# Seven products of an MLP pair in three PSUM banks instead of seven

## The chip, the cores and the metric

The kernel runs on one core of a Trainium2 chip. The time is device microseconds of one execution. The kernel before took 1361.07 us (median of 3 runs, 1359.0 to 1362.8).

## The reference, cut to what matters

The program is one step of a two-layer decoder over 576 tokens (512 of a prompt, 64 of samples), 1024 features wide. A layer ends with an MLP:

```
up = rmsnorm(x, w) @ w_up            # 576 x 1024 times 1024 x 4096
x  = x + square(relu(up)) @ w_down   # 576 x 4096 times 4096 x 1024
```

Everything is float32. The kernel keeps that precision with matmuls of a narrower kind: each operand is split into a high and a low part, and a product is the sum of three matmuls (high times high, high times low, low times high).

## The kernel before, in words

Data lies with features on the 128 partitions and tokens along the free side, in two halves of 288 tokens (`TH`). The 4096 hidden features are 32 tiles of 128. A layer's MLP is a loop over eight chunks of four tiles (`fc` in `mlp`); while a chunk is computed, the chunk before it is multiplied down into x (`down`, line 1018, tile `pd`).

The first six tiles of a layer are computed plainly (`up_tile`, line 336, tile `pu`). The other 26 are taken in 13 pairs (`up_pair`). The 2 x 2 block product of a pair (two tiles of weights, two halves of tokens, the 1024 features in two halves) is done in the Strassen-Winograd way: seven products instead of eight, on sums of weights and sums of inputs. The second chunk holds one pair, and chunks three to eight hold two each. So a layer has one single pair, then six first and six second pairs of a chunk; the last of the second ones has no pair after it.

A product is 12 matmuls of 128 x 288 (four feature blocks, three matmuls each), made by the helper `mul`. The products are p1 to p7. Their right sides are parts of the normed x (`xh`, `xl`) or of the sums `Th`, `Tl`. Their left sides are weights in four kinds of tile: `a` (p1, p2), `s` (p6, p5), `b` (p7, p4), each eight blocks wide and split into `uh`, `ul`, and `d` (p3), four blocks wide, split into `vh`, `vl`. The tag `u` has three buffers, so a, s and b of one pair fill it, and the next pair's a, s and b must each wait until the last matmul on the same buffer is done.

The path of a weight tile: SyncE loads 512 KB into one of three `raw` buffers (line 312); VectorE makes the sums s and the changed ra and rb (lines 1066 to 1069); ScalarE casts the high part (`uh` or `vh`, line 1059); VectorE subtracts to get the low part (`ul` or `vl`, line 1060). When that is done, the raw buffer is free and SyncE may load the next tile.

Each product has a PSUM bank of its own, out of five that rotate (`bank`). ScalarE copies p1 out of its bank (line 1099); VectorE adds the products to what stands in SBUF (line 1089: U = p1 + p6, W = U + p5, p1 + p2, W + p7, U + p7, W + p3, and U with p7 in it + p4). Each of the four sums then gets relu and the norm's factor (line 1092), ScalarE squares it (line 1128) and splits it into high and low (`fh`, line 455; `fl`, line 456).

The order of the instructions on every engine is made by the framework's scheduler when the program is built, from the order of the code, from priorities and from estimates of its own. `high_priority(HP)` puts a piece 3000 places earlier in that ranking. At run time each engine works its list off in that order, and a semaphore wait holds up all that stands behind it on its engine.

Of the kernel before, what the change touches and what calls it, by code (L numbers as in the profile page):

```python
# [14 lines left out]
ALU = mybir.AluOpType  # L15
# [9 lines left out]
TH = T // 2  # L25
# [10 lines left out]
HP = 3000  # L36
# [111 lines left out]
class Kern:  # L148
# [903 lines left out]
    def up_pair(self, P, i, Q, rstd):  # L1052

        nc, V, S, li = self.nc, self.nc.vector, self.nc.scalar, self.li
        ra, rb = (self.raw(self.I["wu"][li, f]) for f in (2 * i, 2 * i + 1))
        hl = lambda n, w, b: (P.t(n + "h", [w, 128], F32R, b), P.t(n + "l", [w, 128], F32R, b))

        def split(hl, src):
            S.copy(hl[0], src)  # L1059
            V.tensor_tensor(hl[1], src, hl[0].bitcast(F32), op=ALU.subtract)  # L1060
            return hl

        with self.tc.high_priority(HP):
            a = split(hl("u", 8, 3), ra)
            s = P.t("s", [8, 128])
            V.tensor_tensor(s[:, :4], rb[:, :4], rb[:, 4:], op=ALU.add)
            V.tensor_tensor(s[:, 4:], s[:, :4], ra[:, :4], op=ALU.subtract)
            V.tensor_tensor(rb[:, :4], ra[:, :4], rb[:, :4], op=ALU.subtract)
            V.tensor_tensor(ra[:, 4:], ra[:, 4:], s[:, 4:], op=ALU.subtract)
            s = split(hl("u", 8, 3), s)  # L1070
            b = split(hl("u", 8, 3), rb)
            d = split(hl("v", 4, 1), ra[:, 4:])

        out = [[self.fp.t(n, dt=F32R, bufs=8) for n in ("fh", "fl")] for _ in range(2)]
        rs = [rstd[:, :TH], rstd[:, TH:]]

        def mul(n, w, o, q):
            ps = self.bank(n)
            j = 0
            for k in range(4):  # L1080
                (wh, wl), (xh, xl) = (t[:, o + k] for t in w), Q[q][k]
                for u, x in ((wh, xh), (wh, xl), (wl, xh)):
                    nc.tensor.matmul(ps[:, :TH], u, x, start=j == 0, stop=j == 11)  # L1083
                    j += 1
            return ps[:, :TH]

        def add(out, x, y):
            with self.tc.high_priority(HP):
                V.tensor_tensor(out, x, y, op=ALU.add)

        def relu(c, m, h):
            V.scalar_tensor_tensor(c, c, 0.0, rs[h], op0=ALU.max, op1=ALU.mult)
            self.square(c, out[m], h)

        U, W = P.t("U", TH), P.t("W", TH)
        p1 = mul("p1", a, 0, "B11")
        c00 = self.half_tile(P)
        with self.tc.high_priority(HP):
            S.copy(c00, p1)
        add(U, c00, mul("p6", s, 4, "T2"))  # L1100
        p5 = mul("p5", s, 0, "T1")
        add(W, U, p5)
        add(c00, c00, mul("p2", a, 4, "B21"))
        relu(c00, 0, 0)
        p7 = mul("p7", b, 0, "T3")
        c11 = self.half_tile(P)
        add(c11, W, p7)
        relu(c11, 1, 1)
        add(U, U, p7)
        c01 = self.half_tile(P)  # L1110
        add(c01, W, mul("p3", d, 0, "B22"))
        relu(c01, 0, 1)
        c10 = self.half_tile(P)
        add(c10, U, mul("p4", b, 4, "T4"))
        relu(c10, 1, 0)
        return out

    def half_tile(self, P=None):
# [256 lines left out]
```

## Time and profile before

| | |
|---|---|
| median of 3 runs | 1361.07 us |
| the profiled execution's own time | 1359.7 us |
| its span | 1357.2 us |
| TensorE busy | 1334.6 us (98%) |
| VectorE busy | 1031.6 us (76%) |
| ScalarE busy | 651.4 us (48%) |

The profile is of one execution. PE is TensorE's matmuls, PEld its weight loads, DVE VectorE, ACT ScalarE, POOL GpSimd and SP SyncE. Matmuls overlap, so their durations (0.29 us here) sum to more than the time that they take; the distance from start to start is what counts. The MLP of layer 0 lies at 292 to 680 us of the span, that of layer 1 at 958 to 1347 us; the first and the last matmul of pairs are at 331 and 629 us in the one, 997 and 1295 us in the other.

### The profile page before, as it was taken

To read this page: it belongs to the slowest core of one execution; us is meant where nothing else is said; L and a number is where in the kernel's file an instruction comes from. 1 tells how busy PE (TensorE), PEld (TensorE's weight loads), DVE (VectorE), ACT (ScalarE), POOL (GpSimd) and SP (SyncE) were. 2 spreads that over 40 slices of the span, in tenths; PEclk is the share of its full clock that TensorE was granted. 3 is DMA by queue.
4 is the path that set the end of the run, shared out by engine and by line. 5 is a ranking of instruction groups with operands and counts; after the bars stand their busy time and mean duration, and the time that the engine had idled before them with its cause. 6 is when DMAs were issued, how large, how long until landed. Compare 5 with 4: busy or idle time off the path is not lost.

```text
span 1357.2 us, 25456 instructions
## 1 busy us (share of the span) xinstructions
PE 1334.6 (98%) x10376; PEld 1287.3 (95%) x10376; DVE 1031.6 (76%) x2059; ACT 651.4 (48%) x1167; POOL 63.7 (5%) x125
## 2 busy tenths in 40 slices
PE   7999999999999999999999999999999999999997
PEld 7898999899999999999998999989999999999997
DVE  7977887498678677777669789766877778677755
ACT  6456446666243234333454653666653243334325
POOL 4020102000000000000100010010000000000000
PEclk9999999999999999999999999999999999999999
DMA  7142424123223232322431332141223223222312
GB/s 262 48 159 105 148 76 143 48 78 110 78 66 106 78 100 72 124 68 82 145 120 37 112 133 80 65 139 61 80 79 125 73 69 109 78 93 79 116 57 70
DMA packets 39716, 131.33 MB, mean 97 GB/s; under 512 B 5960, under 2 KB 8128, under 8 KB 39568
## 3 DMA queue, kind: packets, MB, share of 16 engines
q1 hardware_dynamic: 29312, 102.12, 22.0%
q0 software_dynamic: 6544, 22.65, 4.8%
q10 hardware_dynamic: 3744, 4.95, 1.1%
q8 instruction: 81, 1.33, 0.4%
q14 instruction: 35, 0.29, 0.1%
HBM read 120.32 MB, written 11.34 MB: 97 GB/s over the span
## 4 chain that ended last, share of the span: by engine, by line
PE 92%; DVE 4%; ACT 3%; issue 1%; DMA 0%; DVEq 0%; ACTq 0%
PE pd L336 34%; PE p L1083 21%; PE pi L336 18%; PE pu L336 6%; PE sc L550 2%; PE pl L1235 2%; PE ss L399 1%; PE pdt L336 1%; PE ao L351 1%; PE pt L983 1%; PE o L351 1%; ACT hi L323 1%; PE lg L959 1%; PE y L351 1%; DVE lo L323 0%
## 5 line engine op out<-in xcount | busy, mean ns | idle before, releaser
L336 PE MATMUL pd<-fh,hi 128*128 128x288 f32 x960 | 283.8, 296 | 0.0
L336 PE MATMUL pd<-fl,hi 128*128 128x288 f32 x960 | 283.7, 296 | 0.0
L336 PE MATMUL pd<-fh,lo 128*128 128x288 f32 x960 | 283.6, 295 | 0.0
L323 ACT CAST hi<-raw 128x1024 fp32r<-128x1024 f32 x134 | 140.4, 1048 | 290.4 <-PE pd L336 156.6
L336 PE MATMUL pi<-xh,hi 128*128 128x288 f32 x704 | 210.5, 300 | 7.4 <-ACT xh L374 7.4
L336 PE MATMUL pi<-xl,hi 128*128 128x288 f32 x704 | 211.1, 300 | 0.7 <-DVE xl L375 0.7
L336 PE MATMUL pi<-xh,lo 128*128 128x288 f32 x704 | 210.4, 299 | 0.0
L1018 DVE TENSOR_TENSOR x<-x,pd 128x288 f32<-128x288 f32 x240 | 108.1, 451 | 101.3 <-PE pd L336 101.2
L323 DVE TENSOR_TENSOR lo<-raw,hi 128x1024 fp32r<-128x1024 f32 x134 | 163.9, 1223 | 25.0 <-ACT hi L323 24.1
L336 PEld LDWEIGHTS pd<-fh,hi 128*128 128x128 f32 x960 | 181.1, 189 | 0.0
L336 PEld LDWEIGHTS pd<-fl,hi 128*128 128x128 f32 x960 | 181.0, 189 | 0.0
L336 PEld LDWEIGHTS pd<-fh,lo 128*128 128x128 f32 x960 | 180.6, 188 | 0.0
L336 PEld LDWEIGHTS pi<-xh,hi 128*128 128x128 f32 x704 | 133.1, 190 | 11.1 <-ACT xh L374 7.4
L336 PEld LDWEIGHTS pi<-xh,lo 128*128 128x128 f32 x704 | 133.2, 189 | 3.9 <-issue 3.3
L336 PEld LDWEIGHTS pi<-xl,hi 128*128 128x128 f32 x704 | 133.2, 189 | 3.0 <-DVE xl L375 1.2
L1083 PE MATMUL p<-Th,ul 128*128 128x288 f32 x312 | 92.0, 295 | 0.0
L1083 PE MATMUL p<-Th,uh 128*128 128x288 f32 x312 | 92.0, 295 | 0.0
L1083 PE MATMUL p<-Tl,uh 128*128 128x288 f32 x312 | 92.0, 295 | 0.0
L1083 PE MATMUL p<-xh,ul 128*128 128x288 f32 x312 | 91.9, 294 | 0.0
L1083 PE MATMUL p<-xl,uh 128*128 128x288 f32 x312 | 91.7, 294 | 0.0
L1083 PE MATMUL p<-xh,uh 128*128 128x288 f32 x312 | 91.7, 294 | 0.0
L1059 ACT CAST uh<-raw 128x1024 fp32r<-128x1024 f32 x52 | 54.5, 1047 | 66.6 <-PE p L1083 43.2
(487 smaller groups left out, 3025.5 us busy)
## 6 DMA issues: line engine op xcount, KB each, us to landing
raw<-in_wu SPq DMA_DIRECT2D x64, 512.0 KB, 3.2
raw<-in_wd SPq DMA_DIRECT2D x64, 512.0 KB, 4.4
raw<-in_wi SPq DMA_DIRECT2D x44, 512.0 KB, 3.3
raw<-in_wo SPq DMA_DIRECT2D x16, 512.0 KB, 3.2
x<-in_xT SPq DMA_DIRECT2D x8, 288.0 KB, 6.4
a<-acd ACTq DMA_DIRECT2D x4, 576.0 KB, 4.3
xl<-in_xT POOLq DMA_DIRECT2D x8, 288.0 KB, 4.1
xd<-x POOLq DMA_DIRECT2D x8, 288.0 KB, 2.4
```

The lines of the kernel that those rows point to most:

```text
L323: self.split_ins = nc.scalar.copy(hi, raw).ins, nc.vector.tensor_tensor(lo, raw, hi.bitcast(F32), op=ALU.subtract).ins
L336: self.nc.tensor.matmul(out, w, x[:, a], start=n == 0, stop=n == last)
L351: self.nc.tensor.matmul(out, w, x, start=n < 2, stop=n >= len(products) - 2, skip_group_check=True)
L399: nc.tensor.matmul(ps[:, :TH], ones, s[:, TH * h : TH * h + TH], start=n == 0, stop=n == len(sqs) - 1)
L550: nc.tensor.matmul(pv[:, :, 64 * ci : 64 * ci + 64], kE[:, 128 * ci : 128 * ci + 128], qE[:, :, 64 * ci : 64 * ci + 64], start=True, stop= ...
L959: nc.tensor.matmul(lg[i][:, e, :n], Q[e][kv(i), a], K[kv(i), s0 : s0 + n], start=True, stop=True)
L983: nc.tensor.transpose(pt[:, e, 128 * k : 128 * k + 128], l[:, 128 * k : 128 * k + 128], self.ident)
L1018: self.nc.vector.tensor_tensor(y[:, a], x[:, a], ps, op=ALU.add)
L1059: S.copy(hl[0], src)
L1083: nc.tensor.matmul(ps[:, :TH], u, x, start=j == 0, stop=j == 11)
L1235: nc.tensor.matmul(ps, u[:, o + q], v[:, a], start=j == 0, stop=j == 11)
```

## The change

The seven products go to three banks. In bank A, p1, p6, p5 and p3 are accumulated on top of each other: only p1's first matmul starts the bank anew (`start`), and only p3's last one ends the sum (`stop`). After p1, after p6 and after p5 ScalarE copies what the bank holds to SBUF (`keep`): U1 = p1, U = p1 + p6, W = p1 + p6 + p5. What is in A after p3 is W + p3, one of the four outputs. Bank C takes p7, which is read once for W + p7, and then p4 on top of it, read for U + p7 + p4. Bank B takes p2. The order of the products becomes p1, p2, p6, p7, p5, p3, p4; it was p1, p6, p5, p2, p7, p3, p4.

A pair has three ScalarE copies where it had one, and three VectorE adds where it had seven. The relu step of W + p3 reads the bank itself. U1 is one more SBUF tile of 288 floats per partition, and `dynamic_dma_scratch_size=8192` sets the SBUF kept for descriptors of GpSimd's DMAs, which was left at its default of 16384 bytes.

```diff
-        def mul(n, w, o, q):
-            ps = self.bank(n)
+        def mul(ps, w, o, q, last=True, first=True):
+
             j = 0
             for k in range(4):
                 (wh, wl), (xh, xl) = (t[:, o + k] for t in w), Q[q][k]
                 for u, x in ((wh, xh), (wh, xl), (wl, xh)):
-                    nc.tensor.matmul(ps[:, :TH], u, x, start=j == 0, stop=j == 11)
+                    nc.tensor.matmul(ps, u, x, start=first and j == 0, stop=last and j == 11, skip_group_check=True)
                     j += 1
-            return ps[:, :TH]
-
-        def add(out, x, y):
+
+        def keep(dst, ps):
             with self.tc.high_priority(HP):
-                V.tensor_tensor(out, x, y, op=ALU.add)
-
-        def relu(c, m, h):
-            V.scalar_tensor_tensor(c, c, 0.0, rs[h], op0=ALU.max, op1=ALU.mult)
+                S.copy(dst, ps)
+
+        def done(m, h, x, y=None):
+            c = self.half_tile(P)
+            with self.tc.high_priority(HP):
+                if y is not None:
+                    V.tensor_tensor(c, x, y, op=ALU.add)
+                    x = c
+                V.scalar_tensor_tensor(c, x, 0.0, rs[h], op0=ALU.max, op1=ALU.mult)
             self.square(c, out[m], h)
 
-        U, W = P.t("U", TH), P.t("W", TH)
-        p1 = mul("p1", a, 0, "B11")
-        c00 = self.half_tile(P)
-        with self.tc.high_priority(HP):
-            S.copy(c00, p1)
-        add(U, c00, mul("p6", s, 4, "T2"))
-        p5 = mul("p5", s, 0, "T1")
-        add(W, U, p5)
-        add(c00, c00, mul("p2", a, 4, "B21"))
-        relu(c00, 0, 0)
-        p7 = mul("p7", b, 0, "T3")
-        c11 = self.half_tile(P)
-        add(c11, W, p7)
-        relu(c11, 1, 1)
-        add(U, U, p7)
-        c01 = self.half_tile(P)
-        add(c01, W, mul("p3", d, 0, "B22"))
-        relu(c01, 0, 1)
-        c10 = self.half_tile(P)
-        add(c10, U, mul("p4", b, 4, "T4"))
-        relu(c10, 1, 0)
+
+        A, B, C = (self.bank(n)[:, :TH] for n in ("pA", "pB", "pC"))
+        U1, U, W = P.t("U1", TH), P.t("U", TH), P.t("W", TH)
+        mul(A, a, 0, "B11", last=False)
+        keep(U1, A)
+        mul(B, a, 4, "B21")
+        done(0, 0, U1, B)
+        mul(A, s, 4, "T2", last=False, first=False)
+        keep(U, A)
+        mul(C, b, 0, "T3", last=False)
+        mul(A, s, 0, "T1", last=False, first=False)
+        keep(W, A)
+        done(1, 1, W, C)
+        mul(A, d, 0, "B22", first=False)
+        done(0, 1, A)
+        mul(C, b, 4, "T4", first=False)
+        done(1, 0, U, C)
         return out
...
-    nc = _bacc.Bacc("TRN2", target_bir_lowering=False, num_devices=1)
+    nc = _bacc.Bacc("TRN2", target_bir_lowering=False, num_devices=1, dynamic_dma_scratch_size=8192)
```

TensorE, before, a second pair of a chunk (layer 0, fourth chunk), where p5 ends (bank `p_814`) and p2 begins in another bank:

```order
L1083 MATMUL p_814_5638<-xl_3429,uh_5591 128x288
L1083 MATMUL p_814_5638<-xh_3428,ul_5592 128x288
L1083 MATMUL p_815_5652<-xh_3408,uh_5582 128x288 [waits DVE_49]
L1083 MATMUL p_815_5652<-xl_3409,uh_5582 128x288
L1083 MATMUL p_815_5652<-xh_3408,ul_5583 128x288
```

TensorE, now, the same pair, where p5 ends in bank A (`pA_5577`) and p3 begins in it:

```order
L1083 MATMUL pA_5577<-xl_3429,uh_5561 128x288
L1083 MATMUL pA_5577<-xh_3428,ul_5562 128x288
L336 MATMUL pd_5699<-fh_4890,hi_5695 128x288
L336 MATMUL pd_5699<-fl_4891,hi_5695 128x288
L336 MATMUL pd_5699<-fh_4890,lo_5696 128x288
L336 MATMUL pd_5699<-fh_4892,hi_5695 128x288
L336 MATMUL pd_5699<-fl_4893,hi_5695 128x288
L336 MATMUL pd_5699<-fh_4892,lo_5696 128x288
L1083 MATMUL pA_5577<-xh_3408,vh_5569 128x288 [waits Activation_49]
L1083 MATMUL pA_5577<-xl_3409,vh_5569 128x288
```

The scheduler has moved six matmuls of the down product (`pd`) into the place between p5 and p3, and p3's first matmul has a wait on ScalarE. In the first pair of a chunk ten matmuls of the second pair's p1 stand in that place; in the single pair and in a layer's last pair there are four of `pd`.

ScalarE, before, the same chunk, from the copy of the first pair's p1 (`T1a_5472`) to the copy of the second pair's p1 (`T_5622`); between them stand the casts of the second pair's weights:

```order
L1099 COPY T1a_5472<-p_783_5459 128x288 [waits PE_49]
L1059 CAST uh_5582<-raw_5578 128x1024 [waits DMAHW0_49,DVE_49,PE_49]
L323 CAST hi_5792<-raw_5790 128x1024 [waits DMAHW3_49]
L1059 CAST uh_5591<-s_5586 128x1024 [waits DVE_49,PE_49]
L1059 CAST vh_5599<-raw_5578 128x512 [waits DVE_49,PE_49,Activation_49]
L1059 CAST uh_5595<-raw_5580 128x1024 [waits DMAHW1_49,PE_49]
L1099 COPY T_5622<-p_811_5609 128x288 [waits PE_49]
```

ScalarE, now, in the first pair of that chunk (`pA_5432`), its copies of U and of W:

```order
L1088 COPY U_5436<-pA_5432 128x288 [waits PE_49]
L323 CAST hi_5757<-raw_5755 128x1024 [waits DMAHW3_49]
L1059 CAST uh_5561<-s_5556 128x1024 [waits PE_49]
L1088 COPY W_5437<-pA_5432 128x288 [waits PE_49]
L1059 CAST vh_5569<-raw_5548 128x512 [waits DVE_49,PE_49]
```

And in the second pair (`pA_5577`):

```order
L1059 CAST uh_5565<-raw_5550 128x1024 [waits DMAHW1_49,PE_49]
L1088 COPY U_794_5580<-pA_5577 128x288 [waits PE_49]
L1128 ACTIVATE u_5542<-u_5542 128x288 [waits DVE_49]
L455 CAST fh_5430<-u_5542 128x288 [waits Activation_49]
L1088 COPY U_5581<-pA_5577 128x288 [waits PE_49]
L1128 ACTIVATE T_5608<-T_5608 128x288 [waits DVE_49]
L455 CAST fh_5573<-T_5608 128x288 [waits Activation_49]
L1059 CAST uh_5945<-raw_5941 128x1024 [waits DMAHW6_49]
L1088 COPY W_5582<-pA_5577 128x288 [waits PE_49]
```

The copy of W stands right behind a cast of 1024 elements in both: in the first pair behind the cast of the second pair's s (`uh_5561`, which waits for a matmul), in the second pair behind the cast of the next chunk's first weight tile (`uh_5945`, which waits for its load). Outside the pairs the lists of all engines read as before.

## Rows read from the trace of the kernel before

**Rows 1.** The page: busy time of each engine, share of the span, instructions.

```profile
PE 1334.6 (98%) x10376; PEld 1287.3 (95%) x10376; DVE 1031.6 (76%) x2059; ACT 651.4 (48%) x1167; POOL 63.7 (5%) x125
```

**Rows 2.** PE's waits over the span: waited for, us in total, times, longest.

```profile
PE pi L336 <- ACT xh L374: 7.4, 1, 7.4
PE xt L746 <- DVE b L727: 1.9, 2, 1.5
...
PE sc L550 <- DVE qE L546: 0.3, 1, 0.3
```

**Rows 3.** Busy time in both stretches of pairs: length, engines (instructions), PE clock, DMA, GB/s.

```profile
331.00:660.00 329.00, 329.00 (x2481) 329.00 (x2480) 239.28 (x439) 120.06 (x199) 3.33 (x6) 1.00 0.26 87
1000.00:1290.00 290.00, 290.00 (x2186) 290.00 (x2186) 218.31 (x399) 108.55 (x180) 0.00 (x0) 1.00 0.27 90
```

**Rows 4.** Timeline of PE, a pair's p3, p4 and the next p1: start, us.

```profile
375.88 0.30 PE L1083 MATMUL p<-xh,vh 128*128 128x288 f32 x1
...
377.48 0.30 PE L1083 MATMUL p<-Th,uh 128*128 128x288 f32 x1
...
379.08 0.29 PE L1083 MATMUL p<-xh,uh 128*128 128x288 f32 x1
...
380.53 0.29 PE L1083 MATMUL p<-xh,ul 128*128 128x288 f32 x1
380.65 0.30 PE L1083 MATMUL p<-Th,uh 128*128 128x288 f32 x1
```

**Rows 5.** Timeline of ACT, the copy of that p1.

```profile
380.85 0.40 ACT L1099 COPY u<-p 128x288 f32<-128x288 f32 x1 [0.66 <-PE p L1083]
```

**Rows 6.** Timeline around a start of PE after ACT, late in the span.

```profile
1348.07 0.44 ACT L1245 ACTIVATE sq<-x 128x288 f32<-128x288 f32 x1 [0.58 <-DVE x L1239]
...
1348.56 0.30 PEld L1249 LDWEIGHTS ss<-sq,ones 128*128 128x128 f32 x2 [0.80 <-ACT sq L1245]
```

**Rows 7.** Timeline of PE, a matmul after a short gap and the one behind it.

```profile
778.48 0.40 PE L336 MATMUL pi<-xl,hi 128*128 128x288 f32 x1
778.72 0.29 PE L336 MATMUL pi<-xh,lo 128*128 128x288 f32 x1
```

**Rows 8.** Timeline of ACT, a cast that waited for its load, and what follows it.

```profile
430.49 0.75 ACT L455 CAST fh<-u 128x288 fp32r<-128x288 f32 x2
...
434.05 1.05 ACT L1059 CAST uh<-raw 128x1024 fp32r<-128x1024 f32 x1 [1.47 <-DMA raw<-in_wu]
435.00 0.44 ACT L1128 ACTIVATE T1b<-T1b 128x288 f32<-128x288 f32 x1
```

**Rows 9.** Timelines of DVE and of SP before that cast.

```profile
428.15 1.22 DVE L1060 TENSOR_TENSOR ul<-raw,uh 128x1024 fp32r<-128x1024 f32 x1
429.28 0.82 DVE L1092 SCALAR_TENSOR_TENSOR u<-u,ssq 128x288 f32<-128x288 f32 x2
...
426.76 1.46 SPq L312 DMA_DIRECT2D raw<-in_wd  x2
429.39 0.33 SPq L312 DMA_DIRECT2D raw<-in_wu  x1
```

**Rows 10.** The page's DMA issues: tile, queue, count, KB, median us from issue to landing.

```profile
raw<-in_wu SPq DMA_DIRECT2D x64, 512.0 KB, 3.2
```

**Rows 11.** ACT's waits for that load: us in total, times, longest.

```profile
ACT uh L1059 <- DMA raw<-in_wu: 22.5, 13, 3.5
```

**Rows 12.** Line 1089 on DVE, one of its forms: min/median/max ns.

```profile
L1089 DVE TENSOR_TENSOR U<-U,p x26: 445/447/449, 340.1 to 1292.6; 128x288 f32<-128x288 f32 x26
```

**Rows 13.** The page's queue of GpSimd's DMAs: packets, MB, share.

```profile
q0 software_dynamic: 6544, 22.65, 4.8%
```

## The prediction

> **What bounds the kernel now.** I read the busy times first: TensorE is busy 98% of the span, no other engine over 76% [rows 1]. The list of TensorE's waits has nine rows, 14.3 us in total, and no row of a pair's matmuls (line 1083) is among them [rows 2]. Then the two stretches in which the pairs stand: TensorE is busy in all of 329.0 and all of 290.0 us, at a granted clock of 1.00, with 2481 and 2186 matmuls [rows 3]. That is 0.1326 us from one matmul's start to the next. So in the pairs nothing can be won by waiting less: TensorE waits for nothing. Time changes only if TensorE is made to wait, or if the 0.1326 us change.
>
> **What the change removes.** Four VectorE adds of a pair go, 26 x 4 = 104 instructions of 0.447 us [rows 12], about 46 us of VectorE's busy time. VectorE is busy 239.28 of 329.0 us there [rows 3] and holds up no matmul, so this is worth nothing: TensorE's own stream is the cover, and it stays. Seven banks a pair become three; as no product waited for a bank, that is worth nothing either. The number and shape of matmuls stay. The smaller reserve for GpSimd's transfers touches 6544 packets, 4.8% of the transfer engines' time [rows 13]; nearly all of it lies in the mixers, and I cost it at nothing. If TensorE did wait there, one such wait would be in the size of those that it has, up to 7.4 us [rows 2].
>
> **What it adds.** ScalarE gets two more copies a pair, 52 of 0.40 us [rows 5]: 21 us on an engine that is busy 120.06 of 329.0 us [rows 3]. Their own time is hidden. New is that TensorE waits for them: p6, p5 and p3 go on in bank A and may start only when the copy out of A is done. Behind a waiting matmul the whole of TensorE stands. I work out each of the three waits from one chain. The last matmul of a product starts 0.133 before the place S that follows it, and lasts 0.29. In the trace p1's last matmul starts at 380.53, ends at 380.82, and the copy starts at 380.85 [rows 4, 5]: 0.03 later. The copy takes 0.40. From ScalarE's end to TensorE's next weight load it is 0.05 (1348.07 + 0.44 = 1348.51, load at 1348.56) [rows 6]. After a gap the first matmul shares its time with its weight load: the next one starts 0.24 later (778.48 to 778.72) in place of 0.133 [rows 7], 0.11 more. Together: the sum goes on at S + 0.16 + 0.03 + 0.40 + 0.05 + 0.11 = S + 0.75, if ScalarE is free. What stands between must cover 0.75 us, which takes 5.7 matmuls.
>
> *p6 after the copy of U1, p5 after the copy of U.* Between them stand p2 and p7, 12 matmuls each, 1.59 us: covered, with 0.84 to spare. ScalarE's list puts a cast of 1024 elements ahead of the copy of U1 in second pairs; it is released by the end of p4 of the pair before and eats this margin to about nothing (below 0.02 x 12 = 0.2). I take 0.1 us.
>
> *p3 after the copy of W.* Between p5 and p3 stands only what the scheduler moved there: 4, 10 or 6 matmuls.
>
> Four of `pd`, the single pair and the last pair of each layer, 4 pairs: nothing stands ahead of the copy on ScalarE. 4 x 0.1327 = 0.53, needed 0.75: a wait of 0.22, 4 x 0.22 = 0.9 us.
>
> Ten of the next pair's p1, the first pairs of chunks three to eight, 12 pairs: ahead of the copy stands the cast of the next pair's s. It takes s's buffer, which is free when p5's eleventh matmul is done (the last that reads the high part): that one starts at S - 0.27 and ends at S + 0.03. The cast starts at S + 0.06, and what follows it starts 0.95 later (434.05 to 435.00) [rows 8]: the copy at S + 1.01, done at S + 1.41, p3 at S + 1.41 + 0.16 = S + 1.57. Covered are 1.33. A wait of 0.24, 12 x 0.24 = 2.9 us.
>
> Six of `pd`, the second pairs but the last, 10 pairs: ahead of the copy stands the cast of the next chunk's first weight tile, which waits for its load; the load waits for a raw buffer, and so for VectorE's low part of b. Count from S', the place after p4 of the first pair. b's buffer is free at S' + 0.03; two casts of 288 elements stand ahead on ScalarE (two take 0.75 together [rows 8]), and I let the second hold up the cast of b for 0.3: it starts at S' + 0.36 and ends at S' + 1.41. VectorE, not quite idle, starts the low part near S' + 1.59 and needs 1.22; SyncE issues 0.02 after (429.37 and 429.39) [rows 9]; the load lands 3.2 later [rows 10], at S' + 6.03. Then 0.05, the cast's 0.95, the copy's 0.40, and 0.16 to p3: S' + 7.59. TensorE has 2 + 12 + 12 + 12 + 12 + 6 = 56 matmuls in between, 7.43. A wait of 0.16, 10 x 0.16 = 1.6 us. This is the term with the most play, for it is the difference of two long chains: were VectorE free at once, it would be nothing; at a landing time of 4.6, as where two other loads had just been issued [rows 8, 9], it would be 1.56 a pair.
>
> **The sum.** 0.9 + 2.9 + 1.6 + 0.1 = 5.5 us, and nothing on the other side. The profiled execution took 1359.7 us, so 1365.2; the median of the runs is 1.4 above it, so 1366.6 us, 0.4% slower.
>
> [...]
>
> **Unknown: the matmul's spacing.** Neighbouring products of one shape differ with no wait between them: 375.88 to 377.48 and 377.48 to 379.08 are 1.60 for 12, 0.1333 each; 379.08 to 380.65 is 1.57, 0.1308 [rows 4]. What decides this the trace doesn't show; the change alters which bank follows which, and with the reserve and U1 where tiles lie in SBUF. If the 2184 matmuls of the pairs all went at the one or the other, against 0.1327: -4.1 or +1.3 us. I take 0.
>
> **Rivals.** *The load is late.* In second pairs the cast ahead of the copy of W waits for its load, and each microsecond of lateness is one of TensorE's. For it: ScalarE waited for such loads 13 times, 22.5 us, at most 3.5 [rows 11]. Against: they were loads issued right behind two others [rows 9]. It begins to show once a landing exceeds 3.05 us. At 4.6 in all ten: 10 x 1.56 = 15.6 in place of 1.6, so 1380.6 us.
>
> *The copies are covered after all.* ScalarE may reach its casts and copies some 0.2 us earlier than my chains say, as they are all sums of five or six terms. Then about 0 to 1.5 us remain: 1361.8 us. For it: none of the 26 waits for W that I find is over 0.24 us. Against: the four-matmul case has no unknown in it.
>
> *The spacing falls, and the kernel is faster.* If tiles and banks now lie so that matmuls go at 0.1308 wherever they stand in the program, 10,376 of them [rows 1] save 10,376 x 0.0019 = 19.7 us, less the 5.5: 1346.9 us. It makes the kernel faster by over 0.3% from a fall of 0.9 ns (9.6 us) on. For it: the difference between neighbours above. Against: the mean is the same in both stretches, 329.0 / 2481 = 0.1326 and 290.0 / 2186 = 0.1327 [rows 3], though their tiles differ in part, and the products that now share a bank are the same matmuls on the same operands.
>
> **How the numbers follow.** The forecast 0.62, the late load 0.12, covered copies 0.18, spacing 0.08. Within the forecast the spacing of the pairs alone and play of 0.05 us in each wait spread the time over 1362 to 1371. What measurement can tell from no change is about 0.3%, 4.1 us. The forecast's 5.5 lies near that: I give 0.44 of its 0.62 to slower, 0.18 to the same. So slower 0.44 + 0.12 = 0.56; same 0.18 + 0.18 = 0.36; faster 0.08. The range, 1359 to 1378, leaves out most of the spacing rival and the worst part of the late load; the forecast's own is 1362 to 1371.
>
> **What would show it.** In the profile of the changed kernel TensorE's waits should have rows of line 1083 for ScalarE's `W`, some 26 of them, 0.1 to 0.3 us each and about 5 us in all, and none for `U`; over 1 us each in second pairs would be the late load. VectorE's busy time should fall by about 46 us, ScalarE's rise by 21. A span of the pairs' stretches that is shorter at the same count of matmuls would be the spacing. I am wrong if line 1083 has no waits on ScalarE, or if TensorE's waits grow elsewhere.

## The result, and the profile after the change

| | before | after |
|---|---|---|
| median of the runs | 1360.45 us (8 runs) | 1367.27 us (8 runs) |
| lowest to highest | 1359.0 to 1363.3 | 1365.6 to 1372.2 |
| profiled execution | 1359.7 us, span 1357.2 | 1368.8 us, span 1367.0 |

The ratio is 1.0052, with a 95% interval of 1.0039 to 1.0065: 0.5% slower, 7 us where 5.5 were forecast. The busy line of the page after, against [rows 1]:

```profile
PE 1341.0 (98%) x10376; PEld 1289.2 (94%) x10376; DVE 997.9 (73%) x1955; ACT 672.2 (49%) x1219; POOL 64.4 (5%) x125
```

VectorE has 104 instructions and 33.7 us fewer, ScalarE 52 and 20.8 us more, TensorE the same matmuls, and the time is longer. The same two stretches as [rows 3], in the changed kernel:

```profile
331.00:660.00 329.00, 327.75 (x2450) 325.42 (x2449) 221.24 (x386) 129.75 (x227) 2.85 (x5) 1.00 0.26 86
1000.00:1290.00 290.00, 289.11 (x2162) 287.08 (x2161) 201.15 (x349) 117.95 (x205) 0.00 (x0) 1.00 0.26 88
```

Read the count, not the busy time. PE is still shown busy for nearly all of both stretches, since matmuls lie over each other (0.29 us each, one every 0.133) and a pause under 0.16 us leaves no hole. But 4612 matmuls stand in these 619 us, and 4667 before: 55 fewer, at 0.1327 each 7.3 us. The clock is 1.00 in all four rows. So most of the loss lies in the pairs. Of the 9.1 us between the two profiled executions some 2 lie elsewhere: ahead of the first pair, which begins at 333.3 us here and at 331.3 before. The work there is the same in both kernels, and it varies: in the profile of a kernel whose median is no longer than before (p3 and p4 in banks of their own, below) the first pair begins at 336.6.

TensorE's waits, the list of [rows 2] after the change (a line is: waited for, us in total, times, longest):

```profile
PE pi L336 <- ACT xh L374: 7.5, 1, 7.5
PE xt L746 <- DVE b L727: 2.6, 2, 2.2
PE pA L1083 <- ACT W L1088: 2.1, 2, 1.3
```

The third is new, and it counts only two waits. The rest is found at the other end. The copy's own line (L1088) lists who waited for it, weight loads (PEld) too:

```profile
L1088 ACT COPY U<-pA x52: 382/394/402, 335.2 to 1298.6; 128x288 f32<-128x288 f32 x52
L1088 ACT COPY W<-pA x26: 390/392/399, 341.5 to 1301.8; 128x288 f32<-128x288 f32 x26
...
  PEld pA L1083: 6.3, 19
  PE pA L1083: 2.1, 2
```

Nineteen weight loads waited for a copy, 6.3 us; the two waits of PE lie within these. Which of the two copies they wait for, and what one wait costs, the timeline tells. A first pair, ScalarE's cast of the next pair's s, its copy of W, and TensorE (start, us, engine, line, tiles; in brackets idle before and releaser):

```profile
378.22 1.05 ACT L1059 CAST uh<-s 128x1024 fp32r<-128x1024 f32 x1 [1.46 <-PE pA L1083]
...
379.18 0.39 ACT L1088 COPY W<-pA 128x288 f32<-128x288 f32 x1
...
379.34 0.29 PE L1083 MATMUL pA<-xh,uh 128*128 128x288 f32 x1
379.62 0.19 PEld L1083 LDWEIGHTS pA<-xh,vh 128*128 128x128 f32 x1 [0.22 <-ACT W L1088]
379.62 0.40 PE L1083 MATMUL pA<-xh,vh 128*128 128x288 f32 x1
...
379.86 0.30 PE L1083 MATMUL pA<-xl,vh 128*128 128x288 f32 x1
```

The copy ends at 379.57, p3's first weight load starts at 379.62. From the last matmul ahead (379.34) to p3's first it is 0.28, from that to the second 0.24, where 0.133 is usual: 0.15 + 0.10 = 0.25 us lost.

Summed in this way over the profiled execution (start to start, less 0.133, at the first two matmuls of each), the 26 restarts at p3 lost 7.7 us: 0.23 in each of the 4 pairs with four matmuls between, 0.25 in each of the 12 first pairs, and 3.8 in the 10 second pairs, of which 8 lost 0.07 to 0.22 each and two lost 1.5 and 1.2. At p6, p5, p2, p7 and p4 no start-to-start time is over 0.145. The two large ones are the load. One of them, ScalarE and TensorE, and SyncE's issue of the load:

```profile
578.48 0.33 SPq L312 DMA_DIRECT2D raw<-in_wu  x1
```

```profile
582.14 0.29 PE L1083 MATMUL pA<-xh,ul 128*128 128x288 f32 x1
...
583.08 1.04 ACT L1059 CAST uh<-raw 128x1024 fp32r<-128x1024 f32 x1 [2.58 <-DMA raw<-in_wu]
584.03 0.39 ACT L1088 COPY W<-pA 128x288 f32<-128x288 f32 x1
...
584.47 0.19 PEld L1083 LDWEIGHTS pA<-xh,vh 128*128 128x128 f32 x1 [1.48 <-ACT W L1088]
584.47 0.40 PE L1083 MATMUL pA<-xh,vh 128*128 128x288 f32 x1 [1.25 <-ACT W L1088]
```

The load took 4.6 us from issue to the cast, in place of 3.2. p5, which the copy reads, was complete at 582.43 (the first line is its last matmul; six others stand between it and p3); the copy stood behind a cast for another product's weights.

### The profile page after: what moved, and what is told of

Its sections match the earlier page's. It is cut to its first block, busy times and chain, and to the rows that moved or that the text cites. A ratio compares the mean times of both kernels' runs of the same rounds, so it can differ in the third digit from the quotient of the medians.

```text
span 1367.0 us, 25328 instructions
## 1 busy us (share of the span) xinstructions
PE 1341.0 (98%) x10376; PEld 1289.2 (94%) x10376; DVE 997.9 (73%) x1955; ACT 672.2 (49%) x1219; POOL 64.4 (5%) x125
## 4 chain that ended last, share of the span: by engine, by line
PE 89%; DVE 5%; ACT 4%; issue 1%; DMA 1%; DVEq 0%; ACTq 0%
PE pd L336 34%; PE pi L336 17%; PE pA L1083 12%; PE pu L336 6%; PE pC L1083 6%; PE pB L1083 3%; PE sc L550 2%; PE pl L1235 2%; PE ss L399 1%; PE pdt L336 1%; PE ao L351 1%; ACT hi L323 1%; DMA raw<-in_wu 1%; PE pt L983 1%; PE o L351 1%
## 5 line engine op out<-in xcount | busy, mean ns | idle before, releaser
L1060 DVE TENSOR_TENSOR ul<-raw,uh 128x1024 fp32r<-128x1024 f32 x52 | 63.6, 1223 | 22.5 <-ACT uh L1059 22.5
L336 PE MATMUL pd<-mixh,lo 128*128 128x288 f32 x256 | 77.5, 303 | 0.0
L336 PE MATMUL pd<-mixl,hi 128*128 128x288 f32 x256 | 77.3, 302 | 0.0
L336 PE MATMUL pd<-mixh,hi 128*128 128x288 f32 x256 | 76.9, 302 | 0.0
L1083 PE MATMUL pC<-Th,uh 128*128 128x288 f32 x208 | 61.6, 296 | 0.0
L1083 PE MATMUL pA<-xh,ul 128*128 128x288 f32 x208 | 61.5, 296 | 0.0
```

Of the source, the lines that this page charges most:

```text
L336: self.nc.tensor.matmul(out, w, x[:, a], start=n == 0, stop=n == last)
L1083: nc.tensor.matmul(ps, u, x, start=first and j == 0, stop=last and j == 11, skip_group_check=True)
```

## The experiments

Four questions: is the loss TensorE's wait at p3 and nothing else; is one wait the chain of 0.75 us; what do the reserve and the lighter VectorE weigh; and what is the late load. The matmuls in the same 619 us tell the story of all (the sum of both stretches, as above):

| kernel | matmuls in 619 us | ratio to before, interval |
|---|---|---|
| before | 4667 | |
| after | 4612 | 1.0052 (1.0039 to 1.0065) |
| the reserve alone | 4667 | 1.0002 (0.9990 to 1.0014) |
| p3 in a fourth bank | 4644 | 1.0020 (1.0008 to 1.0033) |
| p3 and p4 in banks of their own | 4666 | 0.9994 (0.9983 to 1.0005) |
| p4 between p5 and p3 | 4665 | 0.9998 (0.9984 to 1.0011) |
| copy ahead of the cast | 4622 | 1.0047 (1.0029 to 1.0065) |
| nothing between p5 and p3 | 4530 | 1.0145 (1.0129 to 1.0162) |
| four raw buffers | 4610 | 1.0052 (1.0039 to 1.0065) |

**p3 in a fourth bank.** The wait is taken away by giving p3 a bank of its own, from which nothing has to be copied first; VectorE adds W to it.

```diff
-        A, B, C = (self.bank(n)[:, :TH] for n in ("pA", "pB", "pC"))
+        A, B, C, D = (self.bank(n)[:, :TH] for n in ("pA", "pB", "pC", "pD"))
...
-        mul(A, s, 0, "T1", last=False, first=False)
+        mul(A, s, 0, "T1", first=False)
...
-        mul(A, d, 0, "B22", first=False)
-        done(0, 1, A)
+        mul(D, d, 0, "B22")
+        done(0, 1, W, D)
```

> p3 gets a fourth bank of its own and W + p3 is a VectorE add again; the copies, the order of products and the small reserve stay. If the loss is TensorE's wait at p3 for the copy of W: no wait of line 1083 on ScalarE, and the time of the kernel before, 1360.5 us within 1.5 (26 VectorE adds more than the changed kernel are hidden). If the loss comes from the new order of products, the reserve or another spacing of the matmuls: 1365 to 1368 us.

Measured: 1363.82 us, somewhat more than half of the loss gone (of the 55 matmuls 32 are back), not all of it: the expectation was missed. No product waits for bank A any more, but p4 now does for bank C. It goes on in p7's bank, which VectorE must have read for W + p7, and that add needs the copy of W. The place of the late load, VectorE and TensorE:

```profile
582.23 1.22 DVE L1060 TENSOR_TENSOR ul<-raw,uh 128x1024 fp32r<-128x1024 f32 x1 [2.81 <-ACT uh L1059]
583.38 0.45 DVE L1094 TENSOR_TENSOR T1b<-W,pC 128x288 f32<-128x288 f32 x1
...
583.88 0.19 PEld L1083 LDWEIGHTS pC<-Th,uh 128*128 128x128 f32 x1 [1.11 <-DVE T1b L1094]
583.88 0.40 PE L1083 MATMUL pC<-Th,uh 128*128 128x288 f32 x1 [0.88 <-DVE T1b L1094]
```

The add came right behind a low part of 1.22 us, which had waited for the cast, which had waited for the load. In all, 22 starts in 18 of the 26 pairs came late at p4, 2.9 us by start-to-start times: 0.11 to 0.12 in each of the 12 first pairs, 0.03 to 0.23 in five second pairs, and 1.15 in this one. In the changed kernel TensorE's wait at p3 had hidden that: there, at the same place, the add of W + p7 came at 585.30, 0.9 us ahead of p4's first matmul at 586.17.

**p3 and p4 in banks of their own.** The same, and p4 in a fifth bank, for which VectorE also adds p7 to U. If the miss was the reuse of bank C, now nothing waits. What changes against the kernel with p3's own bank, without the line that makes the bank E:

```diff
-        mul(C, b, 0, "T3", last=False)
+        mul(C, b, 0, "T3")
...
-        mul(C, b, 4, "T4", first=False)
-        done(1, 0, U, C)
+        with self.tc.high_priority(HP):
+            V.tensor_tensor(U, U, C, op=ALU.add)
+        mul(E, b, 4, "T4")
+        done(1, 0, U, E)
```

> p3 and p4 each get a bank of their own (five banks a pair); p1, p6 and p5 still stack in A with the three copies. With p3 alone in a bank of its own p4 waited for VectorE's W + p7, about 0.12 us in 22 pairs and 1.3 us in one, as it reuses p7's bank. If that is the whole of what was left: no wait of line 1083, 1360.5 us within 1.5. If the three copies or the order of products cost something by themselves: 1362 to 1364 us as with p3's own bank.

Measured: 1359.31 us, not told apart from before, and both stretches are full again:

```profile
331.00:660.00 329.00, 329.00 (x2480) 329.00 (x2479) 232.40 (x417) 132.07 (x230) 2.79 (x5) 1.00 0.27 90
1000.00:1290.00 290.00, 290.00 (x2186) 290.00 (x2185) 209.93 (x374) 120.55 (x208) 0.00 (x0) 1.00 0.26 90
```

No start in the pairs is late. So the loss is waits for a bank, all of it as far as the runs can tell. This kernel keeps the three copies, the smaller reserve, two stacked reuses of bank A, and 52 of the 104 removed adds stay out. Together they neither cost nor win what can be measured.

**p4 between p5 and p3.** Bank A is reused as in the change, but with p4's twelve matmuls as cover (p4 in a bank of its own, U + p7 on VectorE).

```diff
-        A, B, C = (self.bank(n)[:, :TH] for n in ("pA", "pB", "pC"))
+        A, B, C, D = (self.bank(n)[:, :TH] for n in ("pA", "pB", "pC", "pD"))
...
-        mul(C, b, 0, "T3", last=False)
+        mul(C, b, 0, "T3")
         mul(A, s, 0, "T1", last=False, first=False)
         keep(W, A)
         done(1, 1, W, C)
+        with self.tc.high_priority(HP):
+            V.tensor_tensor(U, U, C, op=ALU.add)
+        mul(D, b, 4, "T4")
+        done(1, 0, U, D)
         mul(A, d, 0, "B22", first=False)
         done(0, 1, A)
-        mul(C, b, 4, "T4", first=False)
-        done(1, 0, U, C)
```

> Bank A still takes four products, but p4 goes to a fourth bank and stands between p5 and p3, 12 matmuls; U + p7 is an add of VectorE ahead of it. If it is only the cover that is too short: 1.59 us now cover the 0.75 us (1.57 us behind a cast), so waits near 0 except where a load is late by over 0.8 us, and 1360.5 to 1362 us. If stacking four products in one bank costs something of itself: 1365 to 1368 us.

Measured: 1360.46 us. Only three starts are late, 0.22 us together. Stacking products in one bank costs next to nothing here once twelve matmuls stand between a copy and the next use; VectorE, 28.4 us less busy than before (1003.2 against 1031.6), gives nothing back.

**The copy ahead of the cast.** In the changed kernel's first and second pairs a cast stands ahead of the copy on ScalarE. Here the casts of the next weights are held until the copy of W is issued.

```diff
+            held = lambda on: self.tc.issue_after(self.wcopy) if on and getattr(self, "wcopy", None) is not None else nullcontext()
-            a = split(hl("u", 8, 3), ra)
+            with held(i % 2 == 0):
+                a = split(hl("u", 8, 3), ra)
...
-            s = split(hl("u", 8, 3), s)
+            with held(i % 2 == 1):
+                s = split(hl("u", 8, 3), s)
...
-                S.copy(dst, ps)
+                i = S.copy(dst, ps).ins
+            if dst is W:
+                self.wcopy = i
```

> The copy of W is put ahead of the next pair's cast on ScalarE, in all pairs; the scheduler then leaves four matmuls between p5 and p3 everywhere. If each wait is the chain of 0.75 us less what stands between: 26 waits of 0.22 us, all alike, 5.7 us, 1366.2 us, no late loads and so little spread. If casts and loads ahead of the copy are what costs: about 1 us left, 1361 to 1362 us.

Measured: 1367.44 us. The scheduler now leaves four matmuls in all 26 pairs (as with the 4 pairs before), so the copy came earlier and the cover shrank with it. All 26 waits are alike, 0.23 us, 5.9 us in sum (0.22 and 5.7 were said), and none is large: the copy no longer stands behind a load. Of the copy's line (L1091 here; p3 is L1086), who waited:

```profile
  PEld pA L1086: 5.1, 26
```

**Nothing between p5 and p3.** In addition the matmuls that the scheduler would put between (`pd` and the next pair's p1) are held until p3's first matmul is issued. This measures the chain by itself.

```diff
+    def behind(self):
+        return self.tc.issue_after(self.p3) if getattr(self, "p3", None) is not None else nullcontext()
...
+                    with self.behind() if name == "pd" else nullcontext():
...
+                    if q == "B22" and j == 1:
+                        self.p3 = ins
...
-        mul(A, a, 0, "B11", last=False)
+        with self.behind():
+            mul(A, a, 0, "B11", last=False)
```

> As with the copy of W put ahead of the casts, and nothing may stand between p5 and p3 on TensorE. If TensorE loses the chain from p5's end to p3's restart less what stands between: 26 waits of 0.75 us, 19.5 us, 1380 us. If part of the chain is hidden in some other way (weight loads ahead of their turn, say): under 15 us, below 1375 us.

Measured: 1380.33 us. TensorE's list of waits (its line 1090 is the product, 1097 the copy) and one of the places:

```profile
PE pA L1090 <- ACT W L1097: 12.7, 26, 0.5
```

```profile
381.35 0.40 ACT L1097 COPY W<-pA 128x288 f32<-128x288 f32 x1 [1.59 <-PE pA L1090]
...
381.80 0.19 PEld L1090 LDWEIGHTS pA<-xh,vh 128*128 128x128 f32 x1 [0.72 <-ACT W L1097]
381.81 0.40 PE L1090 MATMUL pA<-xh,vh 128*128 128x288 f32 x1 [0.49 <-ACT W L1097]
```

The copy takes 0.40; then it is 0.05 to the weight load. From p5's last matmul to p3's first it is 0.782 in every pair, and 0.24 to the second: less 0.133 twice, 0.754 lost, 26 times, 19.6 us. The list of waits shows 12.7, because the last matmul's own end (0.29 behind its start) covers the first part of each.

**The reserve alone.** The kernel before, with the one argument of the last hunk (`dynamic_dma_scratch_size=8192`).

> The kernel before with nothing changed but the reserve for GpSimd's descriptors, 8192 bytes. If the loss is the wait at p3: the time of before, 1360.5 us within 1.5, spacing in the pairs 0.1327 us. If the reserve or where tiles lie matters: 1363 to 1367 us, with waits in the mixers or another spacing.

Measured: 1360.92 us, with no late start in the pairs and the matmuls 0.1327 apart as before.

**Four raw buffers.** Does a fourth buffer for the weight loads (and a reserve of 4096, to make room) take the late load away?

```diff
-WRAW, WHL = 3, 2
+WRAW, WHL = 4, 2
```

> The changed kernel with four raw buffers in place of three (and a reserve of 4096 bytes to make room): loads start earlier, and no cast that waits for a load stands ahead of the copy of W; the scheduler leaves ten matmuls between p5 and p3 in 12 pairs and four in 14. If the second pairs' waits were the load: no wait at p3 over 0.3 us is left, 12 x 0.25 + 14 x 0.23 = 6.2 us, 1366.7 us and less spread from run to run. If late waits of over 1 us have another cause, they stay: 1367 to 1369 us.

Measured: 1368.65 us, no better: the second of the two cases. p3 has no wait over 0.26 any more, since no load stands ahead of its copy, as expected (6.3 us in all 26); but a wait of 1.14 turned up at p4, and three other places lost another 0.6 together. ScalarE, VectorE and TensorE there:

```profile
583.84 0.40 ACT L1088 COPY W<-pA 128x288 f32<-128x288 f32 x1 [1.55 <-PE pA L1083]
...
585.20 0.69 DVE L1066 TENSOR_TENSOR s<-raw 128x512 f32<-128x512 f32 x1 [2.39 <-DMA raw<-in_wu]
...
586.54 0.45 DVE L1094 TENSOR_TENSOR T1b<-W,pC 128x288 f32<-128x288 f32 x1
...
587.04 0.19 PEld L1083 LDWEIGHTS pC<-Th,uh 128*128 128x128 f32 x1 [1.11 <-DVE T1b L1094]
```

The copy of W was in time, but the add that frees bank C stood on VectorE behind the first sum of the next pair's weights, which waited for the late load. So the late load reached TensorE by another engine's order. Another load shows the same in a smaller way: p5's restart at 533.65 lost 0.20, behind a copy of U that stood behind a cast that had waited 1.11 for its load.

## Why the prediction came out right

*The base.* TensorE's own stream set the time in the pairs, so the removed work was worth nothing: borne out by the kernels with banks of their own and with p4 between, which do without 52 and 78 of the adds and take the time of before (1359.31 and 1360.46 us against 1360.45). The spacing did not change either: p2's and p7's matmuls, which wait for nothing, stand 0.132 and 0.133 apart, and the mean of all starts in the pairs that are not late is 0.1328 before and after. The rival of a lower spacing is out.

*VectorE's 46 us.* Mis-sized: 33.7. Its busy time counts a stretch once in which two instructions lie over each other, and they do by about 0.09 us ([rows 9]: 428.15 + 1.22 is past 429.28). Here taking instructions out of a run of them saved less than their durations: VectorE's durations sum to 44.4 us less than before, and 10.7 us less of them lie over each other. It was not on the path.

*The chain of 0.75 us.* 0.754 where nothing stands between. Every term was read from the kernel before, where no product waits for a bank, and each held.

*p6 and p5.* Covered by twelve matmuls, as said (no start there over 0.145 us behind the one ahead); the 0.1 us allowed for p6 did not show.

*Four matmuls between.* 0.22 predicted, 0.23 measured, in the 4 pairs and in all 26 of the kernel with the copy ahead.

*Ten between, a cast ahead.* 0.24 predicted, 0.25 measured, 12 times. In the timeline above S is 378.15 (the last of the ten matmuls between started at 379.34, nine steps of 0.1327 behind S): the cast starts at S + 0.07 and the copy at S + 1.03, where S + 0.06 and S + 1.01 were said.

*Six between, a load ahead.* This is the term that failed in size. 0.16 in each of ten pairs were said; eight lost 0.07 to 0.22, with a mean of 0.14, and two lost 1.2 and 1.5. So 3.8 us in place of 1.6. The working for an ordinary landing holds, step for step: in all ten pairs the cast of b starts at S' + 0.33 (0.36 was said), the low part at 1.60 (1.59), and the load is issued at 2.85 (2.83). Then eight loads land within 3.1 to 3.3 and two after 4.2 and 4.6. The rival of a late load came true in two pairs of ten, not all. That is why the forecast's 5.5 became 7.7 in this execution, and the ratio's 7.1 (0.0052 x 1360.5) in the median. The interval of the ratio (5.3 to 8.8 us) would just hold 5.5 too, so the medians by themselves don't show that the late loads cost more than the forecast; the trace does, for one execution. How many loads are late in the others isn't known, and the forecast, which took all ten at the median landing, had no term for one or two.

*The rivals.* "Covered after all" is out: the waits came at their full size. The late load was right in its mechanism and price (each microsecond of lateness is one of TensorE's: the landing took 4.6 in place of 3.2, and the restart lost 1.5 in place of 0.14), with a share of two in ten. The prediction's argument against it did not hold: late loads were to be those issued right behind two others, and the one of 578.48 shared the transfer engines with no other load.

*What would show it.* I named 26 rows in TensorE's waits; there were two, since a wait shorter than what is left of the matmul ahead (0.29 - 0.133, about 0.16 us) makes no idle time on PE. The weight loads' waits, the counts in the stretches and the start-to-start times show the others.

*The price.* The runs put one on using a bank again: 0.754 us a time with nothing between (19.6 in all), 0.23 with four matmuls, next to nothing with twelve (0.22 in all). From 0.754 and 0.1327 some 5.7 matmuls should be enough where nothing holds up the copy; that is an estimate, and no run has just six and a free ScalarE.

## What to carry to other kernels

In this kernel using a bank again costs TensorE the whole way out and back, the tail of the last matmul, the hand-over, the copy, the hand-over and a weight load that nothing hides (0.754 us with nothing between), less what stands between (0.23 is left with four matmuls); with twelve there it cost next to nothing (0.22 us over the 26 pairs together). Count what stands ahead of the copy in its engine's order, and what that in turn waits for: a copy of 0.39 us behind a cast that waited for a load made TensorE wait for the load (1.5 us lost where the load took 4.6). When such a wait is taken away, look at the next reuse of a bank, for the first wait may have been hiding it (2.9 us came up at p4 once p3 had a bank of its own); and where an engine is bound by its own stream, as TensorE here, lighter neighbours won nothing (1360.46 us with VectorE 28.4 us less busy).

## What was not expected of the hardware

The load that came late was not held up as a whole. The transfer engines in the changed kernel, in the 5 us from 578.4, just ahead of its issue at 578.48 (busy tenths and GB/s in 40 slices of 0.125 us, then the queues):

```profile
DMA  0000000095539959989965110000000000000000
GB/s 0 0 0 0 0 0 0 0 262 98 98 98 426 492 229 393 360 360 459 328 262 197 33 33 0 0 33 33 33 33 0 33 33 0 0 0 0 0 0 0
...
q1 hardware_dynamic: 145, 0.52, 32.5%
q8 instruction: 1, 0.02, 1.1%
```

Nearly all of its 512 KB moved in the first 2.7 us; from then on a trickle of mostly 33 GB/s went on for some 1.4 us. The 16 reports of the load's parts, which the trace has as updates of its semaphore, show the same: fifteen came within 0.3 us of each other, the last 1.40 later (1.09 in the other late pair), and the cast waits for the last. In the same stretch the queue "instruction" has one packet. A stretch around an ordinary load (issued at 433.95, 1.55 into the stretch; 3.2 us to landing; the first block is the load before it) has no such packet and no such tail:

```profile
DMA  8999889955100000000094346999949981000000
...
q1 hardware_dynamic: 275, 1.00, 54.6%
```

In the execution of the changed kernel 81 such packets of 16 KB are spread over the span. In each of four traces (the changed kernel, the one before, four raw buffers, copy ahead) take the ten transfers with the largest lag of the last part, out of the 265 of each whose parts can be told apart: 39 of these 40 have such a packet between issue and landing, and 177 of the other 1020. In the kernel before, too, a load at this place (issued at 572.77) took 5.7 us with such a packet beside it, and with two other loads; ScalarE's cast waited 2.58 us for it, and TensorE did not wait. That such a packet delays one part of a load fits all this, but no run took the packets away or moved them, and the rows read here don't tell which of the 16 engines carried one, so it is not shown.
